# Two pads in the on-chip memory: where the moving operands of the dense products lie against their weights

## Chip, core and metric

The kernel runs on one core of a Trainium2 chip. The metric is the device time of one execution in microseconds (us). Engines are named as the profile names them: PE is TensorE's matmul, PEld its weight load, DVE is VectorE, ACT is ScalarE, POOL is GpSimd, SP is SyncE. Every matmul has a stationary operand (the weights, read by PEld) and a moving operand (streamed by PE). Both are read from SBUF, the on-chip memory of 128 partitions; a tile starts at the same byte address in each partition.

## What is computed

A two-layer encoder trunk on 256 tokens of width 2048, in float32. Each layer is an RMSNorm, one wide input projection, a token mixer (centred pooling in layer 0, a chunked gated DeltaNet in layer 1) beside a cross-attention into 256 memory tokens, a SiLU gate, and an output projection added to the residual. Cut to its products:

```python
def reference(x, mem, ...):
    for i in range(2):
        h = rmsnorm(x, norm_w[i])
        kv = rmsnorm(mem, mem_norm_w[i]) @ w_kv_mem[i]     # 256x2048 @ 2048x4096
        proj = h @ w_in                                    # 256x2048 @ 2048x(mixer + query + gate)
        y = concat([mixer(proj), cross_attention(proj, kv)]) * silu(gate(proj))
        x = x + y @ w_out[i]                               # 256x6144 @ 6144x2048
    return rmsnorm(x, final_norm_w)
```

Nearly all of the arithmetic is in these dense products with weights from HBM.

## The kernel before

**Tiling.** A dense product runs as 128x128 blocks of weights against activations that are held transposed, features on the partitions and 256 tokens along the free dimension. So that float32 keeps its precision in the one-pass type float32r, each operand is split into a rounded high part and a remainder, and each block is three matmuls: high weights on high activations, high weights on low activations, low weights on high activations. The three stand in `dense` (L245) and `out_piece` (L425), all through the helper `mm`, whose one call T.matmul is L192; in the trace all of them have that line, so they are told apart by their tiles.

**Weights.** `stage` (L219) takes weights that a DMA of 512 KB brought into a tile `wr`, rounds them to `wh` on ACT (L226) and subtracts on DVE to get `wl` (L228). There are three `wh` and three `wl` buffers of 4096 bytes a partition. `take` (L232) keeps three staged and four fetched ahead. One such unit of eight blocks feeds 24 matmuls.

**Activations.** The moving operands are the tiles `xs` (normed input, L175), `y` (gated output, L422) and `ms` (memory tokens and pooled columns, L354 and L606), each with a high and a low half of 1024 bytes a partition. Only in one place are the roles turned: for the values of the memory tokens (`mem_kv`, L381) `wh` and `wl` stream as 512 columns and `ms` is the stationary operand.

**Other products.** Attention scores, the DeltaNet's triangular inverses and column sums are float32 matmuls, mostly written to PSUM tiles `pa` and `kk`, in between the dense ones; a few others there are float32r (`rows`, `maskr`, `frow`). An order of PE's and SP's instructions is set by the simulated clock of the class `Flow`; it doesn't know addresses.

**Where tiles lie.** The pools fill SBUF from two sides. From the left come `keep` (L163, constants and the residual `xT`) and `work` (L164, with `wr`, `wh`, `wl`), then the layer's pools. From the right comes first `apad`, a tile of A_PAD floats a partition that nothing reads (L166), then `act` (L167, `xs` and `y`), then `mr` with `ms`. The sizes of what lies nearer the edge therefore set the addresses of all that lies further in. All weight tiles and blocks step by multiples of 512 bytes, and so do all the moving tiles and halves; their address modulo 512 is one number for all blocks.

Of the kernel before, what the change touches and what calls it, by code (L numbers as in the profile page):

```python
# [9 lines left out]
F32 = mybir.dt.float32  # L10
# [7 lines left out]
P = 128  # L18
# [15 lines left out]
SQ_BUFS = 3  # L34
SLICE = 2

A_PAD = 96

P_STAGE = 600
P_UA = 600  # L40
# [99 lines left out]
def trunk_kernel(  # L140
# [18 lines left out]
    nc = tc.nc  # L159
# [3 lines left out]
    keep = ctx.enter_context(tc.tile_pool(name="keep", bufs=1))  # L163
    work = ctx.enter_context(tc.tile_pool(name="work", bufs=2))  # L164
    apad = ctx.enter_context(tc.tile_pool(name="apad", bufs=1, side="right"))
    nc.gpsimd.memset(apad.tile([P, A_PAD], F32, name="apad"), 0.0)  # L166
    act = ctx.enter_context(tc.tile_pool(name="act", bufs=1, side="right"))  # L167
# [38 lines left out]
    xT = keep.tile([P, KT, S], F32, name="xT")  # L206
    epsc = keep.tile([P, 1], F32, name="epsc")
    nc.gpsimd.memset(epsc, EPS)

    units, fetched, staged = [], [], []  # L210

# [1187 lines left out]
```

## Time and profile before

| | |
|---|---|
| median of 3 runs | 2525.12 us (2522.1 to 2525.39) |
| the profiled execution | 2533.24 us |
| its span, first to last instruction | 2531.5 us |
| PE busy | 2501.1 us, 99% |
| DVE busy | 1785.2 us, 71% |
| ACT busy | 1237.5 us, 49% |
| DMA | 172 GB/s on the mean |
| granted TensorE clock, mean | 0.996 of full (2.4 GHz) |

The profiled execution was 8.12 us longer than the median of the timed ones. PE's busy time is a union of records that overlap: each matmul's record lasts until its results have drained, while the next one has begun. The busy share thus says that PE never stood idle for long, not that it ran at its best rate. What tells the rate is the number of matmuls in a stretch that holds nothing else.

### The profile page before, as it was taken

The page shows a single profiled execution, that of the slowest core. Times are in us where ns is not written, and L with a number is a line of the kernel's source. Part 1 is how long each engine was busy: PE and PEld are TensorE (multiplying, and loading weights), DVE is VectorE, ACT ScalarE, POOL GpSimd, SP SyncE. Part 2 cuts the span into 40 slices and gives each one's busy share as a digit, 9 for nine tenths or more (in the row PEclk, how much of TensorE's full clock was granted, in tenths as well). Part 3 has the DMA queues.
Part 4 walks back from the last instruction along what each step waited for, and adds up shares of the span by engine and source line. Part 5 has one row for each costly group of instructions (what it writes and reads, how often), then busy time and mean ns, then how long its engine had stood idle before and what let it go on. Part 6 is the DMA issues. An engine that isn't in the chain of part 4 may idle for free.

```text
span 2531.5 us, 53006 instructions
## 1 busy us (share of the span) xinstructions
PE 2501.1 (99%) x21996; PEld 2446.8 (97%) x21996; DVE 1785.2 (71%) x3317; ACT 1237.5 (49%) x1946; POOL 15.6 (1%) x45
## 2 busy tenths in 40 slices
PE   8999999999999999999999999999999999999998
PEld 7999999999999999988999999999999999999998
DVE  6574555657567585674546558979889797979886
ACT  6544444444444444554344446455555555564645
POOL 0000000000000000000000000000000000000000
PEclk9999999999999999999999999999999999999999
DMA  7655455666565555655564545435344443535352
GB/s 245 222 190 168 162 177 169 195 193 199 193 192 194 187 188 185 216 191 191 193 197 159 171 165 169 161 111 171 126 153 146 143 162 129 175 130 167 124 182 101
DMA packets 120817, 436.17 MB, mean 172 GB/s; under 512 B 13728, under 2 KB 13984, under 8 KB 120576
## 3 DMA queue, kind: packets, MB, share of 16 engines
q1 hardware_dynamic: 118080, 426.06, 51.7%
q0 software_dynamic: 1776, 5.64, 0.7%
q8 instruction: 172, 2.82, 0.4%
q10 hardware_dynamic: 720, 1.08, 0.1%
q14 instruction: 69, 0.57, 0.1%
HBM read 430.63 MB, written 2.10 MB: 171 GB/s over the span
## 4 chain that ended last, share of the span: by engine, by line
PE 94%; DVE 4%; ACT 1%; issue 1%; DMA 0%; DVEq 0%
PE pd L192 84%; PE pa L192 9%; DVE wl L228 2%; PE kk L192 1%; ACT wh L226 1%; PE pa L196 0%; DVE itmp L1003 0%; DVE Ti L1009 0%; DVE cacc L805 0%; DVE ms L356 0%; DVE Dg L993 0%; DVE L L995 0%; DVE o L1275 0%; DMA wr<-in_wv_dram 0%; DVE N L1013 0%
## 5 line engine op out<-in xcount | busy, mean ns | idle before, releaser
L228 DVE TENSOR_TENSOR wl<-wr,wh 128x1024 fp32r<-128x1024 f32 x802 | 981.7, 1224 | 568.2 <-ACT wh L226 565.9
L226 ACT CAST wh<-wr 128x1024 fp32r<-128x1024 f32 x802 | 842.7, 1051 | 960.7 <-PE pd L192 782.0
L192 PE MATMUL pd<-xs,wh 128*128 128x256 f32 x7328 | 1306.5, 282 | 3.6 <-DVE gt L419 2.8
L192 PEld LDWEIGHTS pd<-xs,wh 128*128 128x128 f32 x7328 | 1116.9, 189 | 8.5 <-DVE gt L419 3.0
L192 PE MATMUL pd<-xs,wl 128*128 128x256 f32 x3664 | 1021.2, 279 | 0.0
L192 PEld LDWEIGHTS pd<-xs,wl 128*128 128x128 f32 x3664 | 694.2, 189 | 0.4 <-DVE wl L228 0.2
L192 PE MATMUL pd<-y,wh 128*128 128x256 f32 x2944 | 510.9, 278 | 1.2 <-DVE y L266 1.2
L192 PEld LDWEIGHTS pd<-y,wh 128*128 128x128 f32 x2944 | 445.6, 188 | 1.7 <-DVE y L266 1.4
L192 PE MATMUL pd<-y,wl 128*128 128x256 f32 x1472 | 409.0, 278 | 0.0
L192 PEld LDWEIGHTS pd<-y,wl 128*128 128x128 f32 x1472 | 277.8, 189 | 0.5 <-DVE wl L228 0.4
L192 PE MATMUL pd<-ms,wh 128*128 128x256 f32 x1536 | 264.8, 277 | 0.0
L192 PEld LDWEIGHTS pd<-ms,wh 128*128 128x128 f32 x1536 | 232.0, 188 | 0.2
L192 PE MATMUL pd<-ms,wl 128*128 128x256 f32 x768 | 212.7, 277 | 0.0
L192 PE MATMUL pd<-wh,ms 128*128 128x512 f32 x512 | 161.3, 395 | 6.2 <-ACT ms L355 6.2
L192 PEld LDWEIGHTS pd<-ms,wl 128*128 128x128 f32 x768 | 144.7, 188 | 0.0
L805 DVE SCALAR_TENSOR_TENSOR cacc<-cu,small,cacc 128x256 f32<-128x256 f32 x256 | 122.5, 482 | 5.7 <-ACT cacc L803 1.3
L192 PEld LDWEIGHTS pd<-wh,ms 128*128 128x128 f32 x512 | 96.8, 189 | 26.5 <-ACT ms L355 6.2
L455 DVE TENSOR_TENSOR xT<-xT,pd 128x512 f32<-128x512 f32 x140 | 96.1, 686 | 35.7 <-PE pd L192 35.5
L192 PE MATMUL pd<-wl,ms 128*128 128x512 f32 x256 | 101.1, 395 | 0.3 <-DVE wl L228 0.2
L1003 DVE TENSOR_TENSOR itmp<-L,Ti 128x126 f32<-128x126 f32 (+22 forms) x248 | 63.3, 255 | 2.3
L1009 DVE TENSOR_TENSOR Ti<-Ti,itmp 128x126 f32<-128x126 f32 (+22 forms) x248 | 63.3, 255 | 2.2
L265 ACT CAST y<-yf 128x256 fp32r<-128x256 f32 x92 | 35.9, 405 | 55.9 <-DVE yf L533 54.1
(218 smaller groups left out, 1780.9 us busy)
## 6 DMA issues: line engine op xcount, KB each, us to landing
wr<-in_dw_dram SPq DMA_DIRECT2D x258, 512.0 KB, 3.5
wr<-in_pw_dram SPq DMA_DIRECT2D x192, 512.0 KB, 3.5
wr<-in_wo_dram SPq DMA_DIRECT2D x192, 512.0 KB, 3.5
wr<-in_wv_dram SPq DMA_DIRECT2D x64, 512.0 KB, 4.1
wr<-in_wk_dram SPq DMA_DIRECT2D x64, 512.0 KB, 4.2
wr<-in_pg_dram SPq DMA_DIRECT2D x32, 512.0 KB, 3.8
xs<-in_mem_dram SPq DMA_DIRECT2D x8, 256.0 KB, 6.9
xT<-in_x_dram SPq DMA_DIRECT2D x4, 512.0 KB, 5.8
```

What stands on the lines that cost most here:

```text
L192: T.matmul(out, lhsT=lhsT, rhs=rhs, start=start, stop=stop)
L226: A.copy(out=hi, in_=raw)
L228: V.tensor_tensor(out=lo, in0=raw, in1=hi.bitcast(F32), op=ALU.subtract)
L265: A.copy(out=dst[:, 0, :], in_=src)
L455: V.tensor_tensor(out=xv, in0=xv, in1=pss[0], op=ALU.add)
L805: V.scalar_tensor_tensor(out=a, in0=u[:, k : k + S], scalar=cwh[:, ct, k : k + 1], in1=a, op0=ALU.mult, op1=ALU.add)
L1003: V.tensor_tensor(out=tv, in0=L[:, j + 1 : 32, j : j + 1].to_broadcast([P, n, c]), in1=Ti[:, j : j + 1, 0:c].to_broadcast([P, n, c]), op=A ...
L1009: V.tensor_tensor(out=Ti[:, j + 1 : 32, 0:c], in0=Ti[:, j + 1 : 32, 0:c], in1=tv, op=ALU.subtract)
```

## The change

The pad at the right edge shrinks from 96 to 8 floats a partition, and a new tile `kpad` of 8 floats a partition is put into `keep` behind `epsc`. What is read and computed stays as it was.

```diff
-A_PAD = 96
+A_PAD = 8
+K_PAD = 8
...
     epsc = keep.tile([P, 1], F32, name="epsc")
     nc.gpsimd.memset(epsc, EPS)
+    nc.gpsimd.memset(keep.tile([P, K_PAD], F32, name="kpad"), 0.0)
```

Addresses come from the built programs. Everything in `keep` behind `epsc` and everything in `work` moves up by 32 bytes; `xs`, `y` and `ms` move up by 352. Start addresses in bytes, modulo 512 (all blocks of a row agree):

| matmuls | role | before | after |
|---|---|---|---|
| dense, 17,712 of 256 columns | moving `xs`, `y`, `ms` | 96 | 448 |
| | weights `wh`, `wl` | 160 | 192 |
| memory values, 768 of 512 columns | moving `wh`, `wl` | 160 | 192 |
| | weights `ms` | 96 | 448 |
| attention scores | moving `memk`, weights `xq` | 192, 96 | 224, 448 |
| attention outputs | moving `xpt`, weights `memv` | 96, 192 | 448, 224 |
| DeltaNet solves | moving `U`'s partners, weights `U` | 192, 192 | 224, 224 |
| transposes of v | moving `cst`, weights `xn` | 384, 224 | 384, 256 |
| decay rows, 384 columns | moving `rows`, next weights `identr` | 128, 320 | 160, 352 |
| mask, 256 columns | moving `maskr` | 64 | 96 |
| output factors, 256 columns | moving `frow` | 192 | 224 |

So in the dense products the moving operand began 64 bytes below the weights (modulo 512), both at 32 modulo 64, and now begins 256 bytes from them, both at multiples of 64. The DeltaNet's own tiles go the other way, from multiples of 64 to 32 modulo 64, with their distances among each other kept. The order of instructions and their waits on every engine are the same as before, with one more memset on POOL at the start, and `apad`'s memset is of 8 columns instead of 96.

## Rows read from the trace of the kernel before

**Rows 1.** Page, busy time of each engine and the chain that ended last:
```profile
PE 2501.1 (99%) x21996; PEld 2446.8 (97%) x21996; DVE 1785.2 (71%) x3317; ACT 1237.5 (49%) x1946; POOL 15.6 (1%) x45
...
PE 94%; DVE 4%; ACT 1%; issue 1%; DMA 0%; DVEq 0%
```

**Rows 2.** Waits of all engines: who waited for whom, us in total, times, longest:
```profile
ACT wh L226 <- PE pd L192: 782.0, 499, 4.1
...
PE pd L192 <- ACT ms L355: 6.2, 1, 6.2
```

**Rows 3.** Dense matmuls alone, by stretch: width, busy (matmuls), clock, DMA share, GB/s:
```profile
264.00:287.00 23.00, 23.00 (x197) 1.00 0.54 177
316.00:339.00 23.00, 23.00 (x198) 1.00 0.57 182
...
438.00:790.00 352.00, 352.00 (x3108) 1.00 0.60 193
798.00:1056.00 258.00, 258.00 (x2193) 1.00 0.60 195
...
1364.00:1387.00 23.00, 23.00 (x198) 1.00 0.54 173
...
1516.00:1533.00 17.00, 17.00 (x147) 1.00 0.54 180
...
1832.00:1865.00 33.00, 33.00 (x293) 1.00 0.53 176
1947.00:1979.00 32.00, 32.00 (x274) 1.00 0.54 180
...
2417.00:2445.00 28.00, 28.00 (x240) 1.00 0.58 187
2500.00:2519.00 19.00, 19.00 (x163) 1.00 0.16 54
sum 1266.00, PE 1266.00; mean PE 57.55
```

**Rows 4.** Timeline of PE, 700 to 703.6 us: start, length, instruction; thirty matmuls apart:
```profile
699.94 0.39 PE L192 MATMUL pd<-xs,wh 128*128 128x256 f32 x2
...
703.34 0.39 PE L192 MATMUL pd<-xs,wh 128*128 128x256 f32 x2
```

**Rows 5.** The same from 1000 to 1004 us, thirty matmuls apart:
```profile
1000.14 0.40 PE L192 MATMUL pd<-ms,wh 128*128 128x256 f32 x2
...
1003.68 0.40 PE L192 MATMUL pd<-xs,wh 128*128 128x256 f32 x2
```

**Rows 6.** Matmuls with tile wh: count, duration of a record in ns, min/median/max:
```profile
L192 PE MATMUL pd<-xs,wh x7328: 276/276/561, 185.7 to 2519.1; 128*128 128x256 f32 x199
...
L192 PE MATMUL pd<-wh,ms x512: 388/394/795, 6.2 to 1190.7; 128*128 128x512 f32 x171
```

**Rows 7.** The same view for tile rows:
```profile
L192 PE MATMUL pa<-rows,selr x64: 336/341/423, 1556.5 to 2390.7; 128*128 128x384 f32 x64
```

**Rows 8.** The same view for tile frow:
```profile
L192 PE MATMUL pa<-frow,fsel x32: 276/279/382, 1684.7 to 2491.7; 128*128 128x256 f32 x32
```

**Rows 9.** The same view for tile xn (transposes):
```profile
L196 PE MATMUL pa<-cst,xn x64: 270/272/299, 1566.7 to 2406.8; 128*128 128x128 f32 x64
```

**Rows 10.** The same view for tile memk (attention scores):
```profile
L192 PE MATMUL pa<-memk,xq x128: 377/379/379, 208.9 to 1464.0; 128*128 128x256 f32 x128
```

**Rows 11.** Groups by line and shape on PE: count, busy us and mean ns, idle before:
```profile
L192 PE MATMUL pa<-maskr,identr 128*128 128x256 f32 x64 | 18.0, 281 | 0.0
...
L192 PE MATMUL pa<-vt,U 128*128 128x128 f32 x128 | 16.9, 275 | 0.0
```

**Rows 12.** Timeline of all engines at the start, the pad's memset on POOL:
```profile
0.74 0.18 POOL L166 MEMSET apad<- 128x96 f32 x1 [0.29 <-POOLq L1384]
```

## The prediction

> **What bounds the kernel now.** I read the page's busy times and its chain first. PE is busy for 99% of the span, and 94% of the chain that ended last is PE's [rows 1]. The waits say the same from the other side: ACT, which makes the weights ready, waited 782.0 us for PE, while the longest wait of PE itself on that list is 6.2 us [rows 2]. So the time is the number of matmuls times the spacing at which they follow each other, and the change touches no number: order, count and waits stay, only addresses move. Everything hangs on the spacing of 17,712 dense matmuls of 256 columns.
>
> The spacing can be counted in stretches that hold dense matmuls only. A record lasts about 276 ns, so some 2.4 records begun earlier reach into a window and are taken off its count. From 438 to 790 us that gives 352 us / 3105.6 = 113.3 ns; from 798 to 1056 us it gives 258 / 2190.6 = 117.8 ns [rows 3]. The timelines agree: thirty matmuls take 3.40 us at 700 us and 3.54 us at 1000 us, which is 113.3 and 118.0 ns [rows 4, 5]. In these two stretches the granted clock is 1.00 (2.4 GHz), the DMA share is 0.60 and the rate is 193 and 195 GB/s; form, shapes and addresses modulo 512 are the same. **One program text therefore runs at two paces**, and holds each for hundreds of us. Across all 22 windows of that view, 8 are at the slower pace: 264, 316, 798, 1364, 1516, 1947, 2417 and 2500 us. They hold 3610 records in 423 us, less 8 x 2.4 = 19, so 3591 matmuls at 117.8 ns. The other fourteen hold the remaining 1266 - 423 = 843 us [rows 3], which at 113.3 ns is 7440 matmuls. So 3591 of 11,031, or 32.6%, run slow. No other engine's load separates the two paces, so I take it that the two reads of SBUF, the weights of the next block and the moving operand of this one, can fall into step with each other in more than one way.
>
> One tool for short forms: 276 ns of record less 113.3 ns of spacing leaves 163 ns of drain [rows 4, 6]. Taking 163 from a record gives its spacing wherever matmuls follow closely.
>
> **The change, part by part.** *The dense products.* Their moving operand goes from 64 bytes below the weights to 256 from them, and both from 32 modulo 64 to a multiple of 64. The trace holds no stream at that distance, so the price is bounded by the nearest forms.
> - Lower end: the transposes, whose operands are 160 apart, have 272 - 163 = 109 ns for 128 columns [rows 9], and the attention scores, 96 apart, 379 - 163 = 216 ns for 256 columns [rows 10]. These are plain float32, which PE streams at half the pace per column; per unit of streaming time, equal to 256 columns of float32r, they need 109 and 108 ns. With nothing in their way dense matmuls might come down to 109.
> - Upper end: float32r at multiples of 64. `rows` needs 341 - 163 = 178 ns for 384 columns, which is 118.7 for 256 [rows 7]; `frow` 279 - 163 = 116 [rows 8]; `maskr` 281 - 163 = 118 [rows 11]. None has distance 256 from the weights that load meanwhile, but all show that a multiple of 64 alone does not bring 109, and that 118.7 is possible there.
>
> The mean now is 0.674 x 113.3 + 0.326 x 117.8 = 114.8 ns. Between the ends stands 113.3 ns, the pace that two thirds of the same instructions already hold. I take that one: it is the nearest form, and what would have to go is only the state in which the two reads disturb each other more. If how close they lie decides on that state, 256 is the farthest that two addresses can be apart modulo 512. The gain is 0.326 x 17,712 = 5774 matmuls x (117.8 - 113.3) = **26 us**.
>
> *The memory values.* The 768 matmuls of 512 columns have 388 to 394 ns in the record, so 225 to 231 ns of spacing [rows 6]. At the best of these for all, the gain is at most half of 768 x 6 ns, 2 us; at 118.7 per 256 columns they would lose 768 x 8 = 6 us. I take 0.
>
> *The small products.* Some 3500 records are not dense (21,996 less 18,480). Their operands go to other residues: the DeltaNet's tiles leave the multiples of 64 with their distances kept. The trace's own difference between placements in such forms is 275 against 272 ns, for `U` at distance 0 and the transposes at 160 [rows 9, 11]; 3 ns on all of them is 10 us, either way. I take 0, as most keep their distance.
>
> *The pads.* The memset of 96 columns takes 0.18 us on POOL at the start [rows 12], where POOL is busy for 15.6 us in all [rows 1]; the smaller one and a second one lie before any wait for POOL and cost 0. Were that cover gone, it would be 0.2 us.
>
> *What is late next.* Nothing at 113.3. ACT and DVE have 49% and 71% of busy time, DMA about 0.60 of its engines in the dense stretches [rows 1, 3]. A unit of weights feeds 24 matmuls, 2.7 us at 113.3 ns and 2.6 us at 109, which is no squeeze.
>
> **Sum.** The profiled execution took 2533.24 us, of which 2531.5 is span; less 26 it is 2507. It stood 8.1 us above the median of the runs shown, 2525.12; I subtract from that median: 2525 - 26 = **2499 us**, with 2489 to 2510 as the range of this case alone (10 us from the small products).
>
> **The rivals.**
> *All stalls go.* If the distance frees the reads of each other altogether, 114.8 falls to 109: 5.8 x 17,712 = 103 us, 2422 us. For it: the forms at 109 [rows 9, 10]. Against it: they stream at half pace, and every float32r row, at four different placements, has 113 or more [rows 6 to 8, 11]. The Trainium skill, "TensorE: Matmul & The Clock Gate", section "Back-to-back issue gap", gives N/2.4 + 2.5 ns warm, 109 ns for 256 columns; by it 2422 would be the time, and no dense row here shows it.
>
> *Slower: the reads lock at the worse pace.* The place is every dense matmul: if multiples of 64 make both reads ask for the same stretch of memory at the same moment, the state of 117.8 becomes the rule. That price is 11,938 matmuls x 4.5 = 54 us, 2579 us; at the 118.7 of `rows`, 17,712 x 3.9 = 69 us, 2594 us. For it: all three float32r forms at multiples of 64 lie at 116 to 118.7 in the middle of their records [rows 7, 8, 11], and the present placement is the best of those in the trace. Against it: two of them have weights of another kind (one repeated column) or a stream that reads a tile twice. It decides as soon as more than 0.326 of the dense matmuls run at the slower pace; each further tenth costs 8 us.
>
> *Placement does nothing.* Two paces stay in about the present shares, since what starts the slower one may be the matmuls in between; the time stays within 5 us of 2525. For it: both paces exist at one placement [rows 3], so the placement alone doesn't fix the pace. The same section's neighbour, "Part 2: What happens when you issue a matmul" of that page in the Trainium skill, says that PE reads weights and moving operand through two independent ports, so loading the next weights takes no bandwidth from the running matmul; by that no address could matter and the time is 2525. The trace speaks against its strict form, since the same stream holds two paces with the clock at 1.00 [rows 3].
>
> **How the numbers follow.** All at 113.3 ns: 0.32, and it is the likeliest single case, so 2499. All stalls go, or much of them: 0.23. About the present mixture: 0.10. Slower: 0.35, of which 0.12 beyond 2582. A measurement of this kernel can tell about 0.2%, 5 us, from no change. Faster by more: 0.32 + 0.23 = 0.55; within: 0.10; slower by more: 0.35. Cases of both signs hold most of the chance, so the range has to take both in: 2420 from the freed reads to 2582 from the locked slower pace, which leaves out 0.05 below and 0.12 above. The likeliest case's own range is 2489 to 2510.
>
> **What would show it.** In the view of tile wh, the median record of 276 ns tells: 276 with no window at 117.8 is the forecast, 272 the freed reads, 281 the locked slower pace. Windows as in rows 3 show whether a stretch still holds two paces. The forecast is wrong if the spacing of dense matmuls is other than 113.3; it is wrong in its reason if the spacing stays and PE's waits change, or if the paces follow the DMA's or DVE's load.

## The result: slower by 3%

The changed kernel takes 2603.27 us in the median (2602.38 to 2605.38), the kernel before 2525.26 us beside it (2522.1 to 2526.28). The ratio is 1.0304, with a 95% interval from 1.0288 to 1.032. The forecast was 2499 us and its range ended at 2582, so both the sign and the range were wrong. The profiled execution of the changed kernel took 2605.38 us, of which 2603.6 is span, 72.1 us more span than that of before.

PE still bounds the kernel. The page after, busy time of each engine and the chain that ended last:

```profile
PE 2578.5 (99%) x21996; PEld 2527.5 (97%) x21996; DVE 1788.9 (69%) x3317; ACT 1237.2 (48%) x1946; POOL 15.6 (1%) x46
...
PE 97%; DVE 1%; DMA 0%; issue 0%; ACT 0%; POOL 0%; DVEq 0%
```

Against [rows 1], PE has the same 21,996 matmuls and 77.4 us more busy time. DVE and ACT do what they did; their share of the chain fell. The waits, who waited for whom, after:

```profile
ACT wh L228 <- PE pd L193: 839.6, 505, 3.3
...
PE pd L193 <- ACT ms L357: 6.2, 1, 6.2
```

ACT waits 57.6 us longer for PE than in [rows 2], and PE's own longest wait is the same 6.2 us. The change put no wait on PE; PE itself goes slower. Dense matmuls alone, by stretch, after (width, busy and count, clock, DMA share, GB/s):

```profile
460.00:770.00 310.00, 310.00 (x2586) 1.00 0.57 184
800.00:1050.00 250.00, 250.00 (x2085) 1.00 0.56 184
```

With the same 2.4 records taken off as in the prediction, these are 310 us / 2583.6 = 120.0 ns and 250 / 2082.6 = 120.0 ns. Where [rows 3] had 113.3 and 117.8 ns in these stretches, there is now one pace, and it lies above both. The clock is 1.00 in both stretches, and the DMA rate fell from 193 to 184 GB/s, about as much as the pace. The timeline of PE after, thirty matmuls apart (start, length, instruction):

```profile
1000.09 0.40 PE L193 MATMUL pd<-y,wh 128*128 128x256 f32 x2
...
1003.69 0.40 PE L193 MATMUL pd<-y,wh 128*128 128x256 f32 x2
```

That is 3.60 us, where [rows 4, 5] have 3.40 and 3.54. Matmuls with tile wh after (count, duration of a record in ns as min/median/max):

```profile
L193 PE MATMUL pd<-xs,wh x7328: 277/283/469, 190.2 to 2591.4; 128*128 128x256 f32 x199
...
L193 PE MATMUL pd<-wh,ms x512: 387/389/794, 6.2 to 1232.0; 128*128 128x512 f32 x171
```

The median record grew from 276 to 283 ns [rows 6], by the same 7 ns as the spacing; the matmuls of 512 columns, whose operands moved just as far, became shorter, 389 ns for 394.

**Where the 72 us lie.** I took the start of every PE record from both traces and summed the gaps from one start to the next, by what the two matmuls are. Between two dense matmuls, gaps under 130 ns: 1972.2 us before (17,156 gaps, 114.96 ns) and 2062.2 after (17,204 gaps, 119.87 ns), so +90.0. Longer gaps between dense ones, where PE waited or changed its output: 68.2 (285 gaps) and 58.7 (237), so -9.4. Among products of 512 columns: -1.2. At the passage from dense to small products: -4.1. All the rest: -3.1. But for rounding the sum is +72.1, the difference of the spans. Of the 90.0, some 6 us are no loss of pace: 48 gaps went from the longer ones to those under 130 ns. The slower pace itself cost 17,156 x 4.91 ns = 84 us, and 12 came back elsewhere, in parts of 1 to 4 us. The chain's share of DVE fell from 4% to 1% [rows 1], which fits a PE that, being slower, meets fewer late weights.

### The profile page after: what moved, and what is told of

The parts are those of the page before. It is cut to its first block, busy times and chain, and to the rows that moved or that the text cites. A ratio compares the mean times of both kernels' runs of the same rounds, so it can differ in the third digit from the quotient of the medians.

```text
span 2603.6 us, 53007 instructions
## 1 busy us (share of the span) xinstructions
PE 2578.5 (99%) x21996; PEld 2527.5 (97%) x21996; DVE 1788.9 (69%) x3317; ACT 1237.2 (48%) x1946; POOL 15.6 (1%) x46
## 4 chain that ended last, share of the span: by engine, by line
PE 97%; DVE 1%; DMA 0%; issue 0%; ACT 0%; POOL 0%; DVEq 0%
PE pd L193 87%; PE pa L193 9%; PE kk L193 1%; PE pa L197 0%; DVE wl L230 0%; DMA xs<-in_mem_dram 0%; ACT wh L228 0%; DVE o L1277 0%; DMA wr<-in_wv_dram 0%; DVE Dg L995 0%; DVE ms L358 0%; DVE L L997 0%; DVE cacc L807 0%; DVE itmp L1005 0%; DVE yf L1146 0%
## 5 line engine op out<-in xcount | busy, mean ns | idle before, releaser
L193 PE MATMUL pd<-xs,wh 128*128 128x256 f32 x7328 | 1351.5, 286 | 2.8 <-DVE gt L421 2.1
L193 PEld LDWEIGHTS pd<-xs,wh 128*128 128x128 f32 x7328 | 1143.2, 192 | 7.5 <-DVE gt L421 2.3
L193 PE MATMUL pd<-xs,wl 128*128 128x256 f32 x3664 | 1036.4, 283 | 0.0
L193 PEld LDWEIGHTS pd<-xs,wl 128*128 128x128 f32 x3664 | 702.0, 192 | 0.0
L193 PE MATMUL pd<-y,wh 128*128 128x256 f32 x2944 | 533.4, 284 | 2.6 <-DVE gt L421 1.6
L193 PEld LDWEIGHTS pd<-y,wh 128*128 128x128 f32 x2944 | 459.1, 192 | 3.4 <-DVE gt L421 1.8
L193 PE MATMUL pd<-y,wl 128*128 128x256 f32 x1472 | 416.5, 283 | 0.0
L193 PE MATMUL pd<-ms,wh 128*128 128x256 f32 x1536 | 278.0, 283 | 0.0
L193 PEld LDWEIGHTS pd<-ms,wh 128*128 128x128 f32 x1536 | 239.7, 192 | 0.2
```

The source lines that it names most:

```text
L193: T.matmul(out, lhsT=lhsT, rhs=rhs, start=start, stop=stop)
```

## The experiments

My theory after the result: distance 256 is no distance. What counts is how far the moving operand lies from the weights modulo 256 bytes, and the new placement is the tie, at which the two reads would meet at the same addresses. Rivals: the alignment to multiples of 64 does it (the other thing that the change moved), or one of the two pads, or being far from the weights at all. In the end the question was which placement is best and what chooses between two paces.

The runs of the whole kernel, in one table. Moving and weights are start addresses modulo 512, the distance is modulo 256, the record is the median of `xs,wh`, and the spacing is that of the stretch from 460 to 770 us, from its count as above (none of these stretches holds anything but dense matmuls). In the last four rows the record takes in the matmuls with low weights, as both parts lie in one tile `wh`. The runs were timed in several sessions, in which the kernel before had medians from 2525.26 to 2531.47 us; the ratios below are each to the kernel before timed beside the run.

| run | moving | weights | distance | record, ns | spacing, ns | median, us |
|---|---|---|---|---|---|---|
| before | 96 | 160 | 192 | 276 | 113.3 | 2525.26 |
| after | 448 | 192 | 0 | 283 | 120.0 | 2603.27 |
| near_aligned | 128 | 192 | 192 | 276 | 113.3 | 2525.4 |
| far_odd | 416 | 160 | 0 | 283 | 120.0 | 2603.74 |
| pad_right_alone | 448 | 160 | 32 | 280 | 116.7 | 2557.06 |
| pad_left_alone | 96 | 192 | 160 | 280 | 117.4 | 2576.3 |
| best112 | 288 | 176, 432 | 112 | 284 | 120.0 | 2604.85 |
| pair192 | 96 | 160, 416 | 192 | 276 | 113.3 | 2526.02 |
| best180 | 96 | 172, 428 | 180 | 276 | 113.3 | 2524.57 |
| best168 | 96 | 184, 440 | 168 | 278 | 116.7 | 2552.39 |

### Alignment or distance: near_aligned and far_odd

The changed kernel with the old distance, both operands still at multiples of 64:

```diff
-A_PAD = 8
+A_PAD = 88
```

> The kernel after with A_PAD 88 in place of 8: moving operands at 128, weights at 192, so 64 below as before, but both at multiples of 64 as after. DISTANCE: like the kernel before, 2499 to 2545 us, with windows at 113.3 and 117.8 ns. ALIGNMENT: like the kernel after, 2590 to 2610 us, 120 ns throughout.

And the kernel before with the new distance, both operands still at 32 modulo 64:

```diff
-A_PAD = 96
+A_PAD = 16
```

> The kernel before with A_PAD 16 in place of 96: moving operands at 416, weights at 160, so 256 from the weights as after, but both at 32 modulo 64 as before. DISTANCE: like the kernel after, 2590 to 2610 us, 120 ns throughout. ALIGNMENT: like the kernel before, 2499 to 2545 us.

near_aligned gave a ratio to before of 0.999 (0.9976 to 1.0005), far_odd 1.0289 (1.0268 to 1.0311). Tile wh in near_aligned:

```profile
L193 PE MATMUL pd<-xs,wh x7328: 276/276/561, 185.7 to 2510.2; 128*128 128x256 f32 x199
```

and in far_odd:

```profile
L192 PE MATMUL pd<-xs,wh x7328: 274/283/562, 190.0 to 2589.8; 128*128 128x256 f32 x199
```

The medians, 276 and 283 ns, follow the distance and not the alignment; near_aligned also keeps both paces of before. This takes the alignment out, and with it the small tiles that changed their residue.

### The curve over distance: map1

A small kernel with nothing but dense triples: two pairs of weights, `wa` at 160 and `wb` at 192 modulo 512, and sixteen moving tiles 32 bytes apart, `mva` at 224 modulo 512 and so on. Each tile runs 96 matmuls, first without a break, then with two float32 matmuls ahead of each tile.

```diff
+for hi, lo in ws:
+    for rep in range(2):
+        for t in mv:
...
+            for g in range(4):
+                for k in range(HC):
+                    T.matmul(ps, lhsT=hi[:, k, :], rhs=xh, start=k == 0, stop=False)
+                    T.matmul(ps, lhsT=hi[:, k, :], rhs=xl, start=False, stop=False)
+                    T.matmul(ps, lhsT=lo[:, k, :], rhs=xh, start=False, stop=k == HC - 1)
```

> A kernel of matmuls alone: it computes nothing of the reference (its output is x as loaded) and leaves out all the trunk's work. Four passes of 16 moving tiles mva to mvp, each with 96 dense triples' matmuls (256 columns, float32r, the order high-high, high-low, low-high over eight blocks, four times). mva starts at 224 modulo 512 and each next one 32 further, so the sixteen take every residue of 32. Passes 1 and 2 use weights at 160 modulo 512 (32 modulo 64, as before the change), passes 3 and 4 weights at 192 (a multiple of 64, as after it); passes 2 and 4 put two plain float32 matmuls ahead of each tile, since such matmuls stood ahead of the stretches at 117.8 ns before. DISTANCE (only the distance modulo 512 counts): with weights at 160 the tile at 96 (mvm) shows 113.3 or 117.8 ns and the one at 416 (mvg) 120; with weights at 192 the tile at 128 (mvn) 113.3 or 117.8 and the one at 448 (mvh) 120; the two curves are the same one shifted by 32 bytes. ALIGNMENT (multiples of 64 cost): mvg at weights 160 stays at 113 to 118, mvn at weights 192 goes to 120, and tiles at 32 modulo 64 are faster than their neighbours. NEITHER (other addresses of the kernel changed the pace): mvm at 160 and mvh at 192 show the same spacing here.

Windows of map1 in the unbroken pass with weights at 192, one in each of the tiles `mva` to `mvh`, distances 32, 64, 96, 128, 160, 192, 224 and 0 in this order (columns as above):

```profile
391.00:401.00 10.00, 10.00 (x88) 1.00 0.01 2
402.50:412.50 10.00, 10.00 (x87) 1.00 0.01 2
414.00:424.00 10.00, 10.00 (x85) 1.00 0.01 2
425.50:435.50 10.00, 10.00 (x86) 1.00 0.00 0
437.00:447.00 10.00, 10.00 (x87) 1.00 0.01 2
448.00:458.00 10.00, 10.00 (x91) 1.00 0.01 2
459.00:469.00 10.00, 10.00 (x87) 1.00 0.01 2
470.50:480.50 10.00, 10.00 (x86) 1.00 0.00 0
```

Only the sixth window, distance 192, that is 64 below, holds 91 matmuls; all others hold 85 to 88. The DMA share is 0.01 at most, so no transfer has a part in it. From the starts of the records the means are 116.65, 117.79, 119.97, 118.64, 118.65, 113.33, 118.30 and 120.00 ns. The tiles 256 bytes further on repeat these to within 1.3 ns, and so does the pass with weights at 160. Distance 192 held 113.34 in both passes with weights at 160 and in the unbroken pass at 192, but 117.79 at 192 when float32 matmuls ran ahead: the two paces of before, both in the small kernel. So in steps of 32 bytes the period is 256, distance 0 gives 120.0, and before's placement was the best of the eight. But distance 96 is as slow as 0, so my theory of the tie is not borne out: the distance decides here, and why one distance is slow and another not is not shown.

### Finer steps, and two attempts to do better: map2, best112, pair192

map2 is map1 with 32 tiles in steps of 8 bytes, one weight pair at 160, and three passes.

```diff
-    for j in range(16):
+    for j in range(32):
...
+        t = t[:, 2 * j : 2 * j + 512]
```

> The kernel of matmuls alone again (nothing of the reference is computed; its output is x as loaded), with weights at 160 modulo 512 and 32 moving tiles in steps of 8 bytes: tile j, in the order mvax, mvay, mvbx to mvpy, starts at a distance of 32 + 8 j from the weights modulo 256. Three passes: tiles straight behind each other, with two plain float32 matmuls of 256 columns ahead of each, with two of 128 columns ahead of each. PERIOD 256, SMOOTH (the pace follows from how far apart the two reads run): the pace changes gradually, 113.3 ns around mvkx (192), with neighbours at 184 and 200 between 113.3 and 118, and some distance may hold 113.3 in all three passes. LINES OF 32 (only which 32-byte piece a read begins in counts): the four tiles of each piece share the pace, with a step at every fourth tile. FLOOR: if some distance frees the reads altogether, it shows 107 to 110 ns.

No distance came under 113.3 ns. Only 112 joined 192 at that pace, and it settled there in all three passes, while 192 took 117.78 in the third; the neighbours of 192, at 184 and 200, stood at about 120.0. One line of the groups for each of 112 and 184 in map2 (the second matmul of a triple):

```profile
L208 PE MATMUL pd<-mvfx,wah x96: 275/275/282, 129.7 to 903.4; 128*128 128x256 f32 x96
```
```profile
L208 PE MATMUL pd<-mvjy,wah x96: 279/282/290, 232.4 to 1010.7; 128*128 128x256 f32 x96
```

275 against 282 ns, 72 bytes apart: the curve isn't smooth, and being nearer or further doesn't order it.

To put the trunk at 112, best112 reads high and low weights of a unit from one tile, 16 bytes in; pair192 is the same with no shift and the old pad, as control.

```diff
-A_PAD = 96
+A_PAD = 48
+W_SHIFT = 4
...
+    def split_pair(shape):
+        t = wt([P, 2 * HC * P + 64], F32R, "wh", W_SPLIT_BUFS)
+        n = HC * P
+        return [
+            t[:, W_SHIFT + i * n : W_SHIFT + i * n + n].rearrange("p (k c) -> p k c", k=shape[1])
+            for i in range(2)
+        ]
...
-                hi = wt(shape, F32R, "wh", W_SPLIT_BUFS)
+                hi, lo = split_pair(shape)
...
-                lo = wt(shape, F32R, "wl", W_SPLIT_BUFS)
```

> The kernel before with the weights' high and low parts as two halves of one tile of 8448 bytes, read from 16 bytes inside it, and A_PAD 48: moving operands at 288, weights at 176 or 432, so 112 apart modulo 256, which in the second map held 113.3 ns in all three passes. MAP (distance modulo 256 alone): one pace of 113.3 ns from start to end, 2495 to 2503 us. PHASE (the matmuls in between bring any distance into a slower state): stretches at 116 or more remain, 2510 to 2530 us.

> The control for best112: the same joint tile for high and low weights, read from its start, A_PAD 96: moving operands at 96, weights at 160 or 416, 192 apart modulo 256 as before the change. MAP: both paces as before, 2518 to 2532 us. If the joint tile itself is worth something, it shows here.

The control stayed at before's time, 1.0005 (0.9989 to 1.0021), so the joint tile costs nothing. best112 was a miss, outside both of its expected ranges: 1.0315 (1.0293 to 1.0336). Tile wh in best112:

```profile
L201 PE MATMUL pd<-xs,wh x10992: 276/284/471, 191.6 to 2590.7; 128*128 128x256 f32 x200
```

284 ns where map2 had 275 at the same distance. What differs from map2 is that the weights no longer begin at a multiple of 32.

### One pad alone: pad_right_alone and pad_left_alone

```diff
-A_PAD = 96
+A_PAD = 8
```

> One half of the change: A_PAD 8, without kpad. Moving operands at 448, weights at 160: 288 apart modulo 512, 32 modulo 256. MAP: 116.7 to 117.8 ns, so 1.8 to 2.8 ns above the mean before at 15.6 us per ns (the change's 78 us over its 5.0 ns): 2553 to 2570 us. FAR IS BAD (the nearer to 256 modulo 512, the slower): 119 to 120 ns, 2588 to 2604 us.

```diff
+K_PAD = 8
...
+    nc.gpsimd.memset(keep.tile([P, K_PAD], F32, name="kpad"), 0.0)
```

> The other half of the change: kpad, with A_PAD 96. Moving operands at 96, weights at 192: 96 below, 160 modulo 256. MAP: 117.3 to 118.7 ns, 2562 to 2584 us. FAR IS BAD: only 32 bytes farther than before, 2530 to 2545 us.

The ratios are 1.0129 (1.0103 to 1.0156) and 1.0201 (1.0179 to 1.0222). The curve of map1 gives 116.65 to 117.78 ns for distance 32 and 117.36 to 118.65 for 160, and both runs came out as it says. Each pad alone loses. The losses, 32 and 51 us, add up to 83, near the 78 of the whole change, but they are not two costs: near_aligned has the left pad as well and loses nothing. They are two other points of one curve. pad_left_alone lies only 32 bytes from the best place and still loses 51 us, so nearness to it is worth nothing.

### What the load has to do with it: map3

Four passes over 32 tiles in steps of 8 bytes: weights cut to 64 columns, 512 moving columns in one matmul, and twice whole weights that begin 16 bytes past a multiple of 32.

```diff
+                        T.matmul(ps, lhsT=ws[0][i // 2][:, k, 0:64], rhs=t[:, 256 * (i % 2) : 256 * (i % 2) + 256],
...
+                        T.matmul(ps, lhsT=ws[0][i // 2][:, k, :], rhs=t[:, 0:512],
...
+                            T.matmul(ps, lhsT=ws[1][i // 2][:, k, :], rhs=t[:, 256 * (i % 2) : 256 * (i % 2) + 256],
```

> The kernel of matmuls alone (nothing of the reference is computed; its output is x as loaded), 32 moving tiles mvax, mvay, mvbx to mvpy in steps of 8 bytes of distance, in four passes. Pass 1: weights cut to 64 columns, 256 moving columns. Pass 2: weights of 128 columns, 512 moving columns. In both, weights start at 0 modulo 32 and the tile's distance is 8 j modulo 256 (mvax 0). Passes 3 and 4: the usual 128 and 256 columns, with weights at 16 modulo 32 (176) and distance 8 j - 16, so that mvix is 112 apart as in the kernel best112; pass 4 has two plain float32 matmuls ahead of each tile. LOAD (at 120 ns the weight load is what is late; the moving stream itself needs 113.3 ns for 256 columns): pass 1 shows 113.3 ns at every distance, pass 2 shows 226.7 ns at distance 0 (mvax). STREAM (the moving read itself is held up at distance 0): pass 1 shows about 120 ns at mvax, pass 2 at least 233 ns there. For best112: ABSOLUTE (the 32-byte piece in which the weights begin counts beside the distance) says mvix at 118 to 121 ns in both passes; PHASE (the trunk's other matmuls start the slow state) says 113.3 ns at mvix in both.

With half the weights to load, the spacing stayed at 115.55 to 120.72 ns (the first tile, which holds the start of the kernel, aside) and reached 113.3 nowhere. I had thought that a shorter load would leave the stream free for longer; it doesn't. At distance 0 it took 116.67 ns, neither the 113.3 of LOAD nor the 120 of STREAM. Tile `mvax` in map3, at distance 0 from the weights of the second pass (the lines of L213 are 512 columns):

```profile
L213 PE MATMUL pd<-mvax,wah x32: 389/389/400, 378.7 to 389.1; 128*128 128x512 f32 x32
```

and tile `mvhy`, at distance 120:

```profile
L213 PE MATMUL pd<-mvhy,wah x32: 399/403/403, 545.7 to 556.7; 128*128 128x512 f32 x32
```

Spacings are 226.66 and 240.00 ns. At 512 columns the tie is the best place of all 32, and 226.66 is twice 113.33. That is what LOAD had said of this pass, so neither of the two accounts holds as a whole. At 256 columns the same distance is slow, at 120.0. This agrees with the 512-column products of the trunk, which became faster (394 to 389 ns). The passes with weights 16 bytes past a multiple of 32 confirm the miss of best112: distance 112 gives 118.33 and 120.00 there, and the places at 113.3 to 113.5 are 64 and 192. So the weights' position within 32 bytes counts beside the distance.

### Weights at every 4 bytes: map4

Eight weight tiles `wa` to `wh`, 0, 4, ... 28 bytes past a multiple of 32, against moving tiles `mva` to `mvh`, 0, 32, ... 224 bytes from there; five passes each, four of them behind float32 matmuls of 256 columns down to 32.

```diff
+    for at in range(8):
+        t = keep.tile([P, 2 * HC * P + 64], F32R, name="w" + "abcdefgh"[at])
...
+        w = [t[:, at + i * n : at + i * n + n].rearrange("p (k c) -> p k c", k=HC) for i in range(2)]
```

> The kernel of matmuls alone (nothing of the reference is computed; its output is x as loaded). Weights wa to wh begin 0, 4, 8, ... 28 bytes past a multiple of 32, moving tiles mva to mvh at 0, 32, ... 224 from there (modulo 256), each pair in five passes of 48 matmuls: straight on, and behind two plain float32 matmuls of 256, 128, 64 and 32 columns. ABSOLUTE (where in its 32 bytes the weights begin counts beside the distance): the eight weights give eight different curves; mvg with wa (192 apart) takes 113.3 ns in some passes and 117.8 in others; if one pair holds 113.3 ns in all five passes, the trunk with that pair takes 2495 to 2505 us. DISTANCE ALONE (the exact distance modulo 256 sets the pace): the values of the second map at the same distances return, 113.3 at distance 112 (we with mve).

Tile `mvg` in map4, with the weights at 0, 12, 16 and 24 bytes (distances 192, 180, 176 and 168):

```profile
L205 PE MATMUL pd<-mvg,wa x240: 276/276/469, 198.7 to 228.3; 128*128 128x256 f32 x120
...
L205 PE MATMUL pd<-mvg,wd x240: 276/276/468, 933.0 to 962.4; 128*128 128x256 f32 x120
L205 PE MATMUL pd<-mvg,we x240: 276/280/468, 1177.1 to 1207.6; 128*128 128x256 f32 x120
...
L205 PE MATMUL pd<-mvg,wg x240: 275/276/469, 1667.5 to 1696.9; 128*128 128x256 f32 x120
```

The medians are 276 at 192, 180 and 168. By the starts of the records, 192 took 117.78 in one pass and 113.3 in four, while 180 and 168 stood at 113.34 in all five. `we` with `mve`, at distance 112, took about 120.0 in all five, so the distance alone does not set the pace. Again nothing lies below 113.3.

### Placing the trunk at 180 and 168: best180 and best168

```diff
+W_SHIFT = 3
```

on the joint tile of pair192, and 6 for best168.

> The kernel before with the high and low weights of a unit in one tile that is read 12 bytes in: weights at 172 and 428 modulo 512, moving operands at 96 as before, so the moving operand lies 180 from the weights modulo 256 and the weights stand 12 bytes past a multiple of 32. The last map had that place at 113.34 ns in all five passes. MAP (the place alone sets the pace): all dense matmuls at 113.3 ns, one pace, median record 276 with the slower share of about 0.33 gone, 2495 to 2505 us. TRIGGER (the matmuls in between start the slower pace, wherever the tiles lie): two paces stay, 2515 to 2530 us. NEIGHBOURS (other places of the trunk that the map lacked, the third buffer or the low half, decide): anything else, 2550 and more.

> The same with the joint weight tile read 24 bytes in: weights at 184 and 440 modulo 512, moving operands at 96, distance 168 modulo 256, weights 24 bytes past a multiple of 32. The last map had that place at 113.34 ns in all five passes as well. MAP: one pace of 113.3 ns, 2495 to 2505 us, equal to the run at distance 180 within 5 us. TRIGGER: 2515 to 2530 us. NEIGHBOURS: 2550 and more, or the two runs differ by over 10 us.

best180 gave 0.9979 (0.9965 to 0.9994), which is little, and best168 1.0094 (1.0074 to 1.0114), about 50 us above what its expectation took from the map. Windows of dense matmuls in best180:

```profile
98.00:143.00 45.00, 45.00 (x377) 1.00 0.57 187
151.00:186.00 35.00, 35.00 (x311) 1.00 0.60 192
438.00:790.00 352.00, 352.00 (x3107) 1.00 0.61 193
798.00:1034.00 236.00, 236.00 (x2085) 1.00 0.61 196
1182.00:1273.00 91.00, 91.00 (x760) 1.00 0.57 186
```

The second to fourth are at 113.3 to 113.4 ns, and the stretch from 798 us, at 117.8 in the trace of before, is free. The first and the last are 45 us / 374.6 = 120.1 ns and 91 / 757.6 = 120.1. Both are stretches of key products that follow straight on the 512-column products, and both keep 120 to their end, 390 matmuls in layer 0, 768 and the next 204 in layer 1. In layer 0 the next break, four records of one column in float32, ends it, and the pace is 113.4 behind it. So this placement, too, has two paces, and the run lies in the range that its expectation gave for that case. Behind the later breaks, where before's trace has 117.9 ns every other time, it has 113.5 to 114 each time, by the starts. Of that gain, 1362 x 6.7 ns = 9 us go back in the two stretches at 120. The windows of best168 show one that the map lacked:

```profile
460.00:770.00 310.00, 310.00 (x2659) 1.00 0.59 189
```

which is 310 / 2656.6 = 116.7 ns. The short passes of map4 did not find that pace; why the trunk holds it is not shown.

### What chooses the pace: best180_kick and before_kick

Four float32 matmuls of one column (eight records) ahead of the first key product of each layer, written over at once by the product itself; in best180 and in the kernel before.

```diff
+            if kick:
+                for _ in range(4):
+                    T.matmul(ps[:, 0:1], lhsT=ident, rhs=ones, start=True, stop=True)
```

> The kernel with the weights 12 bytes further (distance 180), plus four float32 matmuls of one column ahead of the first key product of the memory tokens in each layer; their result is overwritten at once, so nothing else changes. In the run without them 1362 dense matmuls that follow straight on the 512-column products (390 in layer 0, 768 and 204 in layer 1) stood 120.0 ns apart, up to the first float32 matmuls in between, and 113.3 from there. TRIGGER (the place allows two paces, and what runs just ahead of a stretch chooses one): with the kick all three stretches at 113.3, 1362 x 6.7 ns = 9 us less and 1 us of kicks, 2514 to 2519 us. LASTING (the 120.0 belongs to ms as the moving operand, or to the start of the layer): the stretches stay at 120.0 and the time at 2524 to 2527 us.

> The kernel before with the same four small float32 matmuls ahead of the first key product in each layer. Before, the 390 key matmuls that follow straight on the 512-column products in layer 0 ran at 113.4 ns, and the next stretches, each after a break by four small float32 matmuls, went 117.8 (42 matmuls), 113.3 (336), and later 117.9 and 113.9 in turn. TRIGGER in its strict form (each break turns the pace over): the 390 turn to 117.8, the 42 to 113.4, the 336 to 117.8, and the time moves by under 8 us either way, 2520 to 2535 us. NO TURN (the small matmuls don't choose): the three stretches stay at 113.4, 117.8, 113.3 and the time within 2 us of before.

best180_kick took 2517.38 us, 0.9948 (0.9931 to 0.9965): half a per cent below the kernel before. Windows in best180_kick:

```profile
99.00:142.00 43.00, 43.00 (x382) 1.00 0.60 193
149.00:184.00 35.00, 35.00 (x311) 1.00 0.61 194
...
1180.00:1270.00 90.00, 90.00 (x796) 1.00 0.61 199
```

These are 113.3, 113.4 and 113.4 ns. Eight tiny matmuls, four in each layer, turned 1362 dense ones from 120.0 to 113.3. The moving tile `ms` was not to blame, nor the start of a layer. In before_kick the time stayed, 1.0004 (0.9987 to 1.0021). Its windows of the same stretches, and of one later:

```profile
99.00:142.00 43.00, 43.00 (x382) 1.00 0.62 195
144.00:147.00 3.00, 3.00 (x28) 1.00 0.55 198
149.00:186.00 37.00, 37.00 (x329) 1.00 0.59 193
264.00:287.00 23.00, 23.00 (x196) 1.00 0.57 183
```

The first stays at 43 / 379.6 = 113.3 ns behind the kick, and the later ones keep 117 to 119 and 113.3 as in the run without. So a break does not turn the pace over each time. What happens just ahead of a stretch can choose its pace (best180_kick shows that), but the rule by which it chooses is open, and whether the small matmuls do it or the pause that they bring was not separated. In particular, the starts in the trace of before show 48 matmuls at 117.9 and 48 at 113.9 in turn between breaks of one kind (`xpt,memv`, four records each, from 391 us on), and I can't say why.

Small matmuls are not needed for it either. The longest slow stretch of before, 2204 gaps of 117.78 ns from 797 us on, has dense matmuls right ahead of it, with a pause in which PEld waited 0.2 us for a late `wl`. In the traces of pair192, near_aligned and before_kick, all at distance 192, the same 2204 gaps are 113.34 ns behind pauses of the same kind. Two windows of near_aligned, as in [rows 3]:

```profile
438.00:790.00 352.00, 352.00 (x3109) 1.00 0.60 193
798.00:1056.00 258.00, 256.77 (x2264) 1.00 0.62 202
```

The second has 2264 matmuls where before had 2193. So a part of the slower share that the prediction counted, 2204 x 4.44 ns = 10 us, did not come from the placement alone and was not there in other executions at that distance.

## Why the prediction was wrong

**What bounds the kernel: right.** PE's spacing in the dense products sets the time, nothing waits anew, and the two paces are real: pair192 and map1 reproduce both.

**The price of the dense products: the step that failed.** The prediction took 113.3 ns because "256 is the farthest that two addresses can be apart modulo 512". The spacing at the new distance was the term mis-sized, 120.0 ns for 113.3, with the wrong sign against the 114.8 of before. The modulus was an assumption; it came from the steps of the tiles, not from any row. map1 shows 256, and modulo 256 the new placement is distance 0, at 120.0 ns, which far_odd repeats at another alignment. The rule behind it, that reads further apart disturb each other less, fails as well: modulo 256 the farthest distance is 128, at 118.6 ns, and 96 is as slow as 0. Two more things in the same step would have warned. The rows with which it was bounded had no tie among them that streams like the dense products, so the distance was outside what was known; the pairs with distance 0 in the trace, `U` and its partners, are float32 and show 275 ns in the record [rows 11], which they kept. And the upper end, 118.7 from `rows` [rows 7], was taken as an end though it came from one other form: the true value lay 1.3 ns above it. At 118.7 the prediction had 2594 us; the same sum at 120.0 gives 2525 + 92 = 2617, 14 above the measured 2603: the starts show 84 us for the pace, and other gaps became shorter. The range ended at 2582, below even the prediction's own upper price.

**The rival that came true, with another reason.** "Slower: the reads lock at the worse pace" had the sign, the place (every dense matmul) and what the profile would show, a median record of 281 ns; it is 283. Its reason, multiples of 64, is refuted by near_aligned, and its price was too low: at the 120.0 ns that came, 17,712 x (120.0 - 114.8) is 92 us, of which the starts of the records show 84.

**All stalls go: refuted.** Of all placements measured, in four maps, half the weights included, none went below 113.3 ns for 256 columns, and 512 columns never below 226.66. The 109 ns taken from float32 products was not reached at any placement of this form. The formula of the Trainium skill's "Back-to-back issue gap", in "TensorE: Matmul & The Clock Gate", gives 109 ns for 256 columns, but that section calls it the gap of an isolated matmul and says that in a stream with weight loads both operations set the spacing, which the prediction left out; no run here shows 109.

**Placement does nothing: refuted as a whole.** Moving tiles by multiples of 32 bytes is worth from 2525 to 2604 us. But its half-sentence, that what starts the slower pace may be the matmuls in between, has something to it: best180_kick shows that matmuls ahead of a stretch can change its pace, though the longest slow stretch of before began behind a late weight alone. By the Trainium skill's "Part 2: What happens when you issue a matmul" on that page, with two independent ports for weights and moving operand, no address could matter; the 120.0 against 113.3 ns of far_odd and before disagree.

**The memory values, taken at 0: right.** They gained 1.2 us, within the 2 us that the prediction gave as the most.

**The small products, taken at 0 with 10 us either way: right.** Tile rows and the transposes after, the first two lines of their views:

```profile
L193 PE MATMUL pa<-rows,selr x64: 332/338/423, 1611.7 to 2460.0; 128*128 128x384 f32 x64
```
```profile
L197 PE MATMUL pa<-cst,xn x64: 270/272/301, 1622.2 to 2476.8; 128*128 128x128 f32 x64
```

338 and 272 ns for 341 and 272 [rows 7, 9]; all small products together are 3 us shorter.

**The sum, wrong a second time.** Had the whole trunk gone to 113.3 ns, the time would by my estimate still not have been 2499, but some 2511. best180_kick comes near that case: its dense gaps under 130 ns are 113.69 ns on the mean, 21.0 us less than in the profiled execution of before, its span is 2513.5, and its median 2517.38; the 0.36 ns that its 17,162 gaps still lack are 6 us. The prediction worked out the 26 us from the profiled execution, which had the stretch from 798 to 1056 us at 117.8 ns, and then subtracted them from the median of other executions, 8 us shorter. In those part of the gain was already there: the profiled execution of pair192, with 2525.6 us of span, has that stretch at 113.3 by the starts of its records. Against its own 2533.24 the sum would have been 2507.

## What to carry to other kernels

Where a busy engine runs one kind of instruction at two paces, the pace depends on something that the program text doesn't show, here where two operands lie against each other in SBUF and what happened just ahead; a small kernel that steps through the placements costs one run and would have told the modulus before any sum was made. When no row shows the new value of a parameter, bounds from rows at other values are not bounds, and a period that one has assumed is the first thing to doubt. And a gain that is worked out on one execution is to be subtracted from that execution.

## What the runs showed of the hardware

- With float32r, 128x128 weights loaded for each matmul, and 256 moving columns, the spacing is 113.33 ns at best and up to 123.4 elsewhere. It depends on the distance between moving operand and weights modulo 256 bytes and on the weights' position within 32 bytes (map1, map3, map4). Steps of 8 bytes change it by up to 9 ns (map2). How near the two lie doesn't order it: 0 and 96 take 120.0, 112 and 192 can take 113.3. At the clock of 2.4 GHz that these stretches had, the values 113.33, 116.67 and 120.00 ns are 272, 280 and 288 periods.
- The order of the placements is another for 512 columns: 226.66 ns at distance 0, 228.83 at 64, and 229.95 to 240.00 at all others measured (map3).
- Many placements have two stable paces, each held for hundreds of matmuls: 113.3 and 117.8 at 192, 113.3 and 120.0 at 180. Four float32 matmuls of one column, with the pause that they bring, can move a stretch from the one to the other (best180_kick), and in before the pace changed behind nothing but a pause for a late weight.
- Loading half the weights does not quicken the stream: 115.55 ns was the best with 64 columns of weights (map3).
